# Four pairs instead of three in two w_down passes, a pair's sums over raw blocks, and the first loads of x

## The chip, the cores and the metric

The kernel runs on one core of one Trainium2 chip. Its metric is device time in microseconds, the median of several executions. Beside that there is one execution taken by the hardware profiler, from which all rows of the profile come.

## The reference

One layer of a streaming encoder, float32, 256 tokens of 2048 channels:

```python
xn = rms_norm(h, norm1_g)
proj = xn @ w_in                       # 2048 x 5120: q, k, v, two conv halves
att = diff_attention(q, k, v, lam)     # 4 heads, block-causal, then rms_norm
u = silu(layer_norm(conv31(ga * sigmoid(gg))))
h = h + concat(att, u) @ w_out         # 2048 x 2048
hn = rms_norm(h, norm2_g)
h = h + (silu(hn @ w_gate) * (hn @ w_up)) @ w_down     # hidden width 5632
```

The five weight matrices hold 49 million numbers, some 200 MB. Each is read from HBM while it is used.

## The kernel before

**Products in three terms.** Every float32 operand is split into a high part (rounded to fp32r by ScalarE) and a low part (what is left, by VectorE). A product takes three matmuls: high by high, low by high, high by low. One matmul is 128x128 by 128x512.

**Two kinds of unit in the feed-forward half.** The gate and up products run in blocks j = 0 to 10 of 512 hidden columns, and w_down runs in three passes, behind j=3, j=7 and j=10, since the hidden activations are multiplied as they come. A pass has two w_down blocks, each over two groups of 512 output columns. From j=1 on, all these blocks are made of units, which an order string such as `sgGsgGsUUsUu` lists:

- A plain unit (g or u) takes two 128-row slices of one weight matrix for both halves of the tokens: 12 matmuls. In a lower-case unit VectorE makes the low part of the weights (L351). In an upper-case unit ScalarE writes the negated weights (L345), and a DMA of GpSimd adds the raw weights on top (L346).
- A pair unit (s) takes the 2x2 blocks of two slices by two column groups and multiplies them with seven products instead of eight, in the way of Strassen and Winograd: 7 x 3 = 21 matmuls, where a g and a u unit would need 24. For it the four weight blocks b are loaded in one DMA of 1 MB (`load_pair`, L1051), VectorE forms four sums t (`pair_sums`, L1057 to L1059), ScalarE rounds three raw blocks (`round_raw`, L1064) and the four sums (`round_pair`, L1068), and VectorE makes the low parts of both (`split_pair`, L1072 and L1073). The matmuls are lines 1090 to 1092, those of plain units 1112 and 1117. The activation side has its own seven forms; for w_down they are made by `pair_forms` (L965 to L980), while a plain unit of w_down only needs a high and a low part (L953, L955).

**Banks.** A block sums into eight PSUM banks. Seven products go into seven of them. When a block's last pair is done, a generator is started that forms the results from them (`bank_sums`, L1194 to L1199, on VectorE). It enters the instruction streams at the next `resume()`, of which there are two in a plain unit and four in a pair unit. The next block's first pair writes the same banks, in the order Q6, Q7, Q5, Q1, Q2, Q4, Q3, and must wait until they have been read. The last two banks are read by L1213 (gate and up) or L1247 (w_down).

**Order of issue.** `run_chunks` writes the instruction streams by hand. Ahead of unit t it issues, in this sequence: the low parts up to unit t+3; the raw rounding of pairs up to t+5, if the pair two before lies ahead of t; the pairs' sums up to t+5; the units with a DMA low part up to t+5; the rounding up to t+4; and the loads up to t+9. Then come the unit's matmuls. Each engine and each queue works its stream off in order. A pair's blocks b have two buffers (and so have its high and its low parts), its sums t have one, plain raw weights have four.

**Orders.** Block j=1 has `gugusGsUsGsU`, since its activation forms are made at the last moment, blocks j=2 to 10 have `sgGsgGsUUsUu`, and the w_down blocks of the first two passes `sgGsgGgsuUuUu`. In a pass of w_down the pairs of the list in `DOWN` are pairs of slices (j, half); the other slices are plain.

**The start.** SP's queue loads the weights chunk by chunk, and ahead of chunk c the c-th part of x. Only the head (gains and part 0) and part 1 come through ScalarE's queue. Chunks 0 to 3 are half as wide as the others. Chunks up to 9 share the four raw buffers.

Of the kernel before, what the change touches and what calls it, by code (L numbers as in the profile page):

```python
# [13 lines left out]
F32 = mybir.dt.float32  # L14
F32R = mybir.dt.float32r
# [4 lines left out]
P = 128  # L20
# [65 lines left out]

Q1, Q6, Q7, Q5, Q2, Q4, Q3, QX = range(8)

PRODUCTS = ((Q6, 5, 1), (Q7, 6, 2), (Q5, 4, 3), (Q1, 0, 5), (Q2, 1, 6), (Q4, 2, 0), (Q3, 3, 4))

DOWN = (dict(pairs=((1, 0), (1, 1), (2, 0)), order=("sgGsgGgsuUuUu",) * 2),
        dict(pairs=((4, 0), (4, 1), (5, 0)), order=("sgGsgGgsuUuUu",) * 2),
        dict(pairs=((8, 0), (8, 1), (9, 0)), order=("sGsGgsUUu", "sGsGGsUUu")))

RAW_AHEAD = 5
LOAD_AHEAD, DMA_AHEAD, SUMS_AHEAD, HI_AHEAD, LO_AHEAD = 9, 5, 5, 4, 3


BLOCKS = 2 * KD + 1

TO_TRANSPOSE = 5

# [12 lines left out]
def tile_block(  # L115
# [46 lines left out]
    head = pre.tile([P, NK * N], F32, tag="lod", name="head", bufs=1)[:, : NR + S]  # L162
    act.dma_start(out=head, in_=xt[:, : NR + S])
    x_load(XPARTS[1], act)
    pool.tensor_scalar(cols, head[:, :NR], 1.0, 0.0, ALU.mult, ALU.add)

    act.copy(small.tile([P, 8], F32, tag="rsq", name="first"), neghalf)
# [156 lines left out]
    def load_chunk(c):  # L324
        view = lambda t: t.rearrange("p (k n) -> p k n", n=c["width"])[:, : c["nk"]]
        c["view"] = view
        if c.get("spare_raw"):
            c["raw"] = view(early.tile([P, 4 * N], F32, tag="wb", name="raw")[:, : NK * N])
        else:
            c["raw"] = view(wp.tile([P, NK * N], F32, tag="raw", name="raw", bufs=RAW_BUFS))  # L330
        ks = c["ks"] if "ks" in c else range(c["k0"], c["k0"] + c["nk"])
        c["src"] = src = weights([(c["w"], k, col, n) for k in ks for col, n in c["cols"]])
        sp.dma_start(out=c["raw"].rearrange("p k n -> p (k n)"), in_=src)
# [73 lines left out]
            start(c["done"](ps))  # L407

    loaded, rounded, parted = [0], set(), set()
    pair_at, two_at = [], []  # L410

    def earlier(at, i, n):
# [61 lines left out]
    def run_chunks():  # L474
        n = len(chunks)
        pair_at.extend(i for i, c in enumerate(chunks) if "sides" in c)
        two_at.extend(i for i, c in enumerate(chunks) if "kind" in c and "sides" not in c)
        at = dict(part=0, dma=0, sums=0, round=0, minus=0, raw=0)
        first = next(i for i, c in enumerate(chunks) if "kind" in c)

        def until(what, do, stop, only=lambda c: True, may=lambda i: True):
            while at[what] < min(n, stop) and may(at[what]):
                if only(chunks[at[what]]):
                    do(at[what])
                at[what] += 1

        for t in range(n):
            if t >= first - AHEAD:
                until("part", part_of, t + 1 + LO_AHEAD)
                until("raw", lambda i: round_raw(chunks[i]), t + 1 + RAW_AHEAD, lambda c: "sides" in c,  # L490
                      lambda i: i <= t or may_round_raw(t, i))
                until("sums", sums_of, t + 1 + (SUMS_AHEAD if t >= first else 0), may=may_sum)
                until("dma", round_of, t + 1 + DMA_AHEAD, lambda c: c["by_dma"])
                until("round", round_of, t + 1 + (HI_AHEAD if t >= first else LO_AHEAD))
                load_until(t + 1 + LOAD_AHEAD)
            else:
                if t < len(XPARTS):
                    until("part", part_of, t + 2)
                else:
                    until("part", part_of, t + 1 + AHEAD)  # L500
                    until("minus", minus_of, min(t + 1 + MINUS_AHEAD, first), lambda c: c.get("minus"))
                    until("round", round_of, min(t + 1 + ROUND_AHEAD, first))
            part_of(t)
            chunks[t]["multiply"](chunks[t])
            if chunks[t].get("prompt") and chunks[t]["done"]:
                resume()
        while running:
            resume()
# [331 lines left out]
    def out_done(n, ps):  # L840
        cs = slice(n * N, (n + 1) * N)
        for m in range(NM):
            dve.tensor_tensor(h[m][:, cs], h[m][:, cs], ps[m], ALU.add)
        for m in range(NM):
            pool.dma_start(out=out[m * P : (m + 1) * P, cs], in_=h[m][:, cs])
        if n == 2:
            held[0] -= NM
        yield
        for t in range(0, N // P, 2):
            k = n * (N // P) + t  # L850
            yield from room(1)
            pt = aux_ps.tile([P, 2, S], F32, tag="aux", name="ps_h")
            for i in range(2):
                for m in range(NM):
                    pe.transpose(pt[:, i, m * P : (m + 1) * P], h[m][:, (k + i) * P : (k + i + 1) * P], ident)
            if k % HK == 0:
                hn.append(early.tile([P, HK, S], F32, tag="wb", name="hn"))
            rows = hn[k // HK][:, k % HK : k % HK + 2, :]
            for i in range(2):
                act.activation(rows[:, i, :], pt[:, i, :], AF.Copy, scale=col("g2", k + i))  # L860
            hi, lo = lhs_two("h", k)
            act.copy(hi, rows)
            dve.tensor_tensor(lo, rows, hi.bitcast(F32), ALU.subtract)
            for i in range(2):
                hT[k + i] = (hi[:, i, :], lo[:, i, :])
            yield
        for m in range(NM):
            square_sum(h[m][:, cs], ss2[m][:, n : n + 1])
        if n == D // N - 1:
            yield  # L870
            for m in range(NM):
                ss = small.tile([P, 1], F32, tag="ssh", name="ssh")
                dve.tensor_reduce(ss, ss2[m], AX.X, ALU.add)
                rsqrt_mean(rstd2[m], ss, D, EPS)
            yield
            yield
            prestack.close()
            ffn["pool"] = fp = ctx.enter_context(tc.tile_pool(name="ffn", bufs=1))
            spare_lhs.extend(fp.tile([P, 2, 2, S], F32R, tag=f"a{x}", name=f"a{x}") for x in ("hi", "lo"))
            start(make_forms())  # L880


# [40 lines left out]
    def place(g):  # L923
# [3 lines left out]
        fhi, flo = (a[:, :at].rearrange("p (f q) c -> p f q c", f=7) for a in arena)  # L927
        twos = [(j, t) for j in range(sum(FGROUPS[:g]), sum(FGROUPS[: g + 1])) for t in range(2) if (j, t) not in pairs]
        free = [arena_two(i) for i in range(at, BLOCKS - 3, 4)]
        free += [tuple(a[:, i] for a in spare_lhs) for i in range(2)]  # L930
        assert len(free) >= len(twos)
        down[g] = dict(forms=(fhi, flo), pairs=pairs, twos=twos, at=dict(zip(twos, free)), ready=set())

# [107 lines left out]
    def load_pair(c):  # L1041
        if "b" in c:
            return
        queue = sp
        if c is chunks[pair_at[0]]:
            c["b"] = ffn["pool"].tile([P, 7, N], F32, tag="wl", name="wb0", bufs=2)[:, :4]
            queue = pool
        else:
            c["b"] = early.tile([P, 4, N], F32, tag="wb", name="wb")
        src = weights([(w, k, col, N) for w, col in c["sides"] for k in c["ks"]])  # L1050
        queue.dma_start(out=c["b"].rearrange("p k n -> p (k n)"), in_=src)  # L1051

    def pair_sums(c):

        b = c["b"]
        c["t"] = t = ffn["pool"].tile([P, 4, N], F32, tag="wt", name="wt")
        dve.tensor_tensor(t[:, 2:4], b[:, 1:3], b[:, 0:1].to_broadcast([P, 2, N]), ALU.subtract)  # L1057
        dve.tensor_tensor(t[:, 1], b[:, 1], t[:, 3], ALU.add)
        dve.tensor_tensor(t[:, 0], t[:, 1], b[:, 3], ALU.subtract)  # L1059

    def round_raw(c):
        if "hi" not in c:
            c["hi"] = ffn["pool"].tile([P, 7, N], F32R, tag="wh", name="wh", bufs=2)
            act.copy(c["hi"][:, 4:], c["b"][:, 1:])  # L1064

    def round_pair(c):
        round_raw(c)
        act.copy(c["hi"][:, :4], c["t"])  # L1068

    def split_pair(c):  # L1070
        c["lo"] = ffn["pool"].tile([P, 7, N], F32R, tag="wl", name="wl", bufs=2)
        dve.tensor_tensor(c["lo"][:, 4:], c["b"][:, 1:], c["hi"][:, 4:].bitcast(F32), ALU.subtract)  # L1072
        dve.tensor_tensor(c["lo"][:, :4], c["t"], c["hi"][:, :4].bitcast(F32), ALU.subtract)  # L1073

    def sum_bank(c, i):
        sums = c["sums"]
# [145 lines left out]
    def down_products(n, q, last):  # L1222
        so_far = None
        if last:
            so_far = ffn["pool"].tile([P, 4, N], F32, tag="wt", name="so_far")[:, :NM]
            pool.dma_start(out=so_far, in_=out[:, n * N : (n + 1) * N].rearrange("(m p) n -> p m n", p=P))
        bank_sums(q)
        for m in range(NM):
# [42 lines left out]
    for ks, first, last in ((range(0, 4), True, False), (range(4, 6), False, False), (range(6, 8), False, False),  # L1271
                            (range(8, 16), False, True)):
        for n in range(3):
            block("w_out", n * N, ks, fm, (lambda ps, n=n: out_done(n, ps)) if last else None,
                  bkey=("o", n), first=first, last=last, spare=n == 2)
    block("w_out", 3 * N, range(16), fm, lambda ps: out_done(3, ps))
    for i, c in enumerate(chunks[len(XPARTS) : -12]):
        c["spare_raw"] = i % 3 == 2
        c["minus"] = i >= MINUS_FROM and i % 6 == 4
# [12 lines left out]
        j0 += nb  # L1292

    for c, part in enumerate(XPARTS):
        before[c] = lambda c=c, part=part: (x_load(part, sp) if c > 1 else None, x_part(part))
    before[H_FROM + NM - 1] = lambda part=XPARTS[H_FROM + NM - 1]: (x_load(part, sp), x_part(part), start(x_rest()))
    for i in range(2 * NM):
        x_first = before.get(H_FROM + i, lambda: None)
# [40 lines left out]
```

## Time and profile before

| | us |
|---|---|
| median of 3 executions (lowest, highest) | 1037.16 (1037.03, 1037.67) |
| the profiled execution's own time | 1037.66 |
| its span in the profile | 1035.9 |
| granted TensorE clock over the span | 1.00 |
| busy: TensorE, its weight loads, VectorE, ScalarE, GpSimd | 1028.0, 849.0, 862.7, 685.8, 155.1 |

In rows of the profile PE is TensorE, PEld its weight loads, DVE VectorE, ACT ScalarE, POOL GpSimd, and SPq the DMA queue of SyncE. `L1072` is line 1072 of the kernel. A row of the timeline gives start and duration in us, engine, line, operation, output and inputs, shapes, count, and in brackets the idle time of the engine ahead of it with what ended it. Stretches (windows) are in us from the start of the span.

### The profile page before, as it was taken

What the parts mean: (1) busy time and instruction counts of PE and PEld (TensorE: products, weight loads), DVE (VectorE), ACT (ScalarE), POOL (GpSimd) and SP (SyncE); (2) the same over time, 40 slices, a digit from 0 to 9 for tenths busy, and PEclk for the clock granted to TensorE, in tenths of its full rate; (3) what the DMA queues carried; (4) which work ended last, traced back from release to release, by engine and by line L of the source; (5) the groups of instructions that cost most, each with busy time, mean ns of one, the idle gap of its engine ahead of it and who ended that gap; (6) DMA issues with size and microseconds to landing.
All of it is one profiled execution on the core that took longest, in us unless ns stands there. A gap on an engine that the chain in (4) does not pass through costs nothing.

```text
span 1035.9 us, 13050 instructions
## 1 busy us (share of the span) xinstructions
PE 1028.0 (99%) x4641; PEld 849.0 (82%) x4641; DVE 862.7 (83%) x1087; ACT 685.8 (66%) x865; POOL 155.1 (15%) x198
## 2 busy tenths in 40 slices
PE   9999999999999999999999999999999999999998
PEld 7888888888888888788888888888888888888886
DVE  6699889897646699999978779999896697998983
ACT  6855567767756577777566667776765666767761
POOL 0040232411100101011011111110101121111121
PEclk9999999999999999999999999999999999999999
DMA  9967775676566669798889998987969999889896
GB/s 341 326 201 239 236 208 187 189 218 183 154 211 224 229 238 262 247 319 240 254 255 292 260 308 263 307 237 241 309 186 286 290 283 327 234 250 299 238 263 130
DMA packets 66065, 258.05 MB, mean 249 GB/s; under 512 B 7376, under 2 KB 8912, under 8 KB 58576
## 3 DMA queue, kind: packets, MB, share of 16 engines
q1 hardware_dynamic: 48944, 201.34, 53.7%
q0 software_dynamic: 16768, 55.58, 28.2%
q8 instruction: 36, 0.59, 0.2%
q10 hardware_dynamic: 288, 0.29, 0.1%
q14 instruction: 29, 0.24, 0.1%
HBM read 248.80 MB, written 8.39 MB: 248 GB/s over the span
## 4 chain that ended last, share of the span: by engine, by line
PE 83%; DVE 9%; DMA 3%; POOL 2%; ACT 1%; issue 1%; DVEq 0%; ACTq 0%
PE q L1112 23%; PE q L1117 12%; PE q L1090 9%; PE q L1091 9%; PE q L1092 9%; PE acc L387 6%; PE acc L381 6%; PE acc L382 6%; DVE y L592 5%; DVE wlo L351 3%; DMA raw<-in_wts_dram 3%; PE ps_a L918 1%; POOL rsq L220 1%; PE ps_s L727 1%; PE ps_o L805 1%
## 5 line engine op out<-in xcount | busy, mean ns | idle before, releaser
L342 ACT CAST whi<-raw 128x1024 fp32r<-128x1024 f32 (+1 forms) x262 | 270.5, 1042 | 102.8 <-PE acc L382 44.4
L351 DVE TENSOR_TENSOR wlo<-raw,whi 128x1024 fp32r<-128x1024 f32 (+1 forms) x174 | 209.1, 1210 | 71.4 <-ACT whi L342 68.4
L381 PE MATMUL acc<-whi,lhi 128*128 128x512 f32 x416 | 164.2, 395 | 1.2 <-ACT whi L342 1.2
L382 PE MATMUL acc<-whi,llo 128*128 128x512 f32 x416 | 162.2, 390 | 0.0
L1073 DVE TENSOR_TENSOR wl<-wt,wh 128x2048 fp32r<-128x2048 f32 x58 | 132.7, 2287 | 20.2 <-ACT wh L1068 20.1
L1064 ACT CAST wh<-wb 128x1536 fp32r<-128x1536 f32 x58 | 86.0, 1484 | 86.9 <-PE q L1091 54.0
L346 POOL DMA_DIRECT2D wlo<-in_wts_dram x74 | 65.1, 891 | 509.7 <-ACT wlo L345 486.0
L1068 ACT CAST wh<-wt 128x2048 fp32r<-128x2048 f32 x58 | 110.5, 1904 | 18.5 <-DVE wt L1059 18.4
L1090 PE MATMUL q<-wh,fhi 128*128 128x512 f32 x280 | 109.1, 390 | 0.4 <-DVE sum L1197 0.4
L1092 PE MATMUL q<-wl,fhi 128*128 128x512 f32 x280 | 109.0, 389 | 0.0
L1091 PE MATMUL q<-wh,flo 128*128 128x512 f32 x280 | 108.9, 389 | 0.0
L1072 DVE TENSOR_TENSOR wl<-wb,wh 128x1536 fp32r<-128x1536 f32 x58 | 101.6, 1751 | 2.1 <-ACT wh L1064 2.1
L592 DVE SCALAR_TENSOR_TENSOR y<-upad,cw,y 128x256 f32<-128x256 f32 x240 | 100.5, 481 | 3.2 <-ACT y L585 3.2
L387 PE MATMUL acc<-wlo,lhi 128*128 128x512 f32 x368 | 100.7, 395 | 0.5 <-DVE wlo L351 0.5
L381 PEld LDWEIGHTS acc<-whi,lhi 128*128 128x128 f32 x416 | 78.1, 188 | 18.4 <-ACT whi L342 2.3
L382 PEld LDWEIGHTS acc<-whi,llo 128*128 128x128 f32 x416 | 78.2, 188 | 16.0
L1117 PE MATMUL q<-wlo,chi 128*128 128x512 f32 x320 | 86.9, 393 | 0.0
L1112 PE MATMUL q<-whi,chi 128*128 128x512 f32 x320 | 85.8, 390 | 0.0
L1112 PE MATMUL q<-whi,clo 128*128 128x512 f32 x320 | 85.6, 389 | 0.0
L387 PEld LDWEIGHTS acc<-wlo,lhi 128*128 128x128 f32 x368 | 68.4, 188 | 14.6 <-DVE wlo L351 0.9
L345 ACT ACTIVATE wlo<-raw 128x1024 fp32r<-128x1024 f32 x74 | 78.2, 1056 | 0.0
L1057 DVE TENSOR_TENSOR wt<-wb 128x1024 f32<-128x1024 f32 x58 | 70.8, 1220 | 2.0 <-DMA wb<-in_wts_dram 1.6
(224 smaller groups left out, 1682.0 us busy)
## 6 DMA issues: line engine op xcount, KB each, us to landing
raw<-in_wts_dram SPq DMA_DIRECT2D x258, 512.0 KB, 5.6
wb<-in_wts_dram SPq DMA_DIRECT2D x57, 1024.0 KB, 7.9
wlo<-in_wts_dram POOLq DMA_DIRECT2D x74, 512.0 KB, 9.3
lod<-in_wts_dram POOLq DMA_DIRECT2D x14, 512.0 KB, 6.4
out_dram<-sum POOLq DMA_DIRECT2D x22, 256.0 KB, 7.2
h<-in_x_dram SPq DMA_DIRECT2D x4, 512.0 KB, 9.1
out_dram<-h POOLq DMA_DIRECT2D x8, 256.0 KB, 3.7
xt<-in_xt_dram SPq DMA_DIRECT2D x6, 256.0 KB, 6.8
```

The lines of the kernel that those rows point to most:

```text
L342: act.copy(c["hi"], c["raw"])
L351: dve.tensor_tensor(c["lo"], c["raw"], c["hi"].bitcast(F32), ALU.subtract)
L381: pe.matmul(ps[m], xhi[:, ms], hi[:, j, :], start=c["first"] and j == 0, stop=False)
L382: pe.matmul(ps[m], xlo[:, ms], hi[:, j, :], start=False, stop=False)
L387: pe.matmul(ps[m], xhi[:, ms], lo[:, j, :], start=False, stop=c["last"] and j == nk - 1)
L592: dve.scalar_tensor_tensor(y[:, ct, :], src, wk, y[:, ct, :], ALU.mult, ALU.add)
L1073: dve.tensor_tensor(c["lo"][:, :4], c["t"], c["hi"][:, :4].bitcast(F32), ALU.subtract)
L1090: pe.matmul(ps, fhi[:, f, p, :], c["hi"][:, w], start=bool(first), stop=False)
L1091: pe.matmul(ps, flo[:, f, p, :], c["hi"][:, w], start=False, stop=False)
L1092: pe.matmul(ps, fhi[:, f, p, :], c["lo"][:, w], start=False, stop=bool(last))
L1112: pe.matmul(ps, plain[i][e][:, ms], hi[:, i, :], stop=False, start=i == e == 0 and bool(c["first"].get(qs[m])))
L1117: pe.matmul(sum_bank(c, qs[m]), plain[i][0][:, ms], lo[:, i, :], start=False, stop=i == 1 and bool(c["last"].get(qs[m])))
```

## The change

- `DOWN`: the first two passes of w_down have four pairs each, the slices of j=1 and j=2 (and of j=4 and j=5) in both halves, where the second half of j=2 (and of j=5) was plain. The order becomes `sgGsgGsuUsUu`: 4 pair units and 8 plain units, for 3 and 10. Each column group keeps two lower-case and two upper-case plain units, where it had three and two.
- A pair's sums: only two of the four go into t (which is half as big). The third is written over the raw block b[0], and the fourth over b[1], after that block has been rounded and split. For it the blocks are loaded in another order, and the seven forms of the weights stand at other places (`PRODUCTS`). The split of the three raw blocks with the fourth sum is a function of its own, `split_raw`. It is issued with the rounding, if the pair two before stands ahead of the current unit, and with the rest of the split otherwise. The rounding of the four sums becomes two casts, one of t and one of b[0] and b[1], and their split becomes two operations.
- Memory: the space that t gives up goes to a third spare buffer for plain activations (`SPARE`), and the arena of activation parts is one block shorter.
- The start: parts 2 and 3 of x are loaded in one DMA on ScalarE's queue, and the raw weights of chunks 4 and 5 go to the space of v, which is not yet in use then.

```diff
-PRODUCTS = ((Q6, 5, 1), (Q7, 6, 2), (Q5, 4, 3), (Q1, 0, 5), (Q2, 1, 6), (Q4, 2, 0), (Q3, 3, 4))
-
-DOWN = (dict(pairs=((1, 0), (1, 1), (2, 0)), order=("sgGsgGgsuUuUu",) * 2),
-        dict(pairs=((4, 0), (4, 1), (5, 0)), order=("sgGsgGgsuUuUu",) * 2),
+PRODUCTS = ((Q6, 5, 2), (Q7, 6, 0), (Q5, 4, 1), (Q1, 0, 6), (Q2, 1, 4), (Q4, 2, 3), (Q3, 3, 5))
+
+DOWN = (dict(pairs=((1, 0), (1, 1), (2, 0), (2, 1)), order=("sgGsgGsuUsUu",) * 2),
+        dict(pairs=((4, 0), (4, 1), (5, 0), (5, 1)), order=("sgGsgGsuUsUu",) * 2),
         dict(pairs=((8, 0), (8, 1), (9, 0)), order=("sGsGgsUUu", "sGsGGsUUu")))
...
-BLOCKS = 2 * KD + 1
+BLOCKS = 2 * KD
+
+SPARE = 3
...
     x_load(XPARTS[1], act)
+    x_load(range(2, 4), act)
...
+        elif "raw_tag" in c:
+            c["raw"] = view(pre.tile([P, NK * N], F32, tag=c["raw_tag"], name="raw", bufs=1))
...
-        src = weights([(w, k, col, N) for w, col in c["sides"] for k in c["ks"]])
+        blocks = [(w, k, col, N) for w, col in c["sides"] for k in c["ks"]]
+        src = weights([blocks[i] for i in (0, 3, 1, 2)])
...
     def pair_sums(c):
         b = c["b"]
-        c["t"] = t = ffn["pool"].tile([P, 4, N], F32, tag="wt", name="wt")
-        dve.tensor_tensor(t[:, 2:4], b[:, 1:3], b[:, 0:1].to_broadcast([P, 2, N]), ALU.subtract)
-        dve.tensor_tensor(t[:, 1], b[:, 1], t[:, 3], ALU.add)
-        dve.tensor_tensor(t[:, 0], t[:, 1], b[:, 3], ALU.subtract)
+        c["t"] = t = ffn["pool"].tile([P, 2, N], F32, tag="wt", name="wt")
+        dve.tensor_tensor(t, b[:, 2:], b[:, 0:1].to_broadcast([P, 2, N]), ALU.subtract)
+        dve.tensor_tensor(b[:, 0], b[:, 2], t[:, 1], ALU.add)
...
+    def split_raw(c):
+        if "lo" not in c:
+            b = c["b"]
+            c["lo"] = ffn["pool"].tile([P, 7, N], F32R, tag="wl", name="wl", bufs=2)
+            dve.tensor_tensor(c["lo"][:, 4:], b[:, 1:], c["hi"][:, 4:].bitcast(F32), ALU.subtract)
+            dve.tensor_tensor(b[:, 1], b[:, 0], b[:, 1], ALU.subtract)
+
     def round_pair(c):
         round_raw(c)
-        act.copy(c["hi"][:, :4], c["t"])
+        act.copy(c["hi"][:, :2], c["t"])
+        o = earlier(pair_at, c["at"], 2)
+        if o is None or o < now[0]:
+            split_raw(c)

     def split_pair(c):
-        c["lo"] = ffn["pool"].tile([P, 7, N], F32R, tag="wl", name="wl", bufs=2)
-        dve.tensor_tensor(c["lo"][:, 4:], c["b"][:, 1:], c["hi"][:, 4:].bitcast(F32), ALU.subtract)
-        dve.tensor_tensor(c["lo"][:, :4], c["t"], c["hi"][:, :4].bitcast(F32), ALU.subtract)
+        split_raw(c)
+        act.copy(c["hi"][:, 2:4], c["b"][:, :2])
+        dve.tensor_tensor(c["lo"][:, :2], c["t"], c["hi"][:, :2].bitcast(F32), ALU.subtract)
+        dve.tensor_tensor(c["lo"][:, 2:4], c["b"][:, :2], c["hi"][:, 2:4].bitcast(F32), ALU.subtract)
...
+    for m in range(NM):
+        chunks[RAW_BUFS + m]["raw_tag"] = f"v{m}"
...
-        before[c] = lambda c=c, part=part: (x_load(part, sp) if c > 1 else None, x_part(part))
+        before[c] = lambda c=c, part=part: (x_load(part, sp) if c > 3 else None, x_part(part))
```

More of the change, by code (lines that the diff above doesn't have):

```diff
@@ L409, in tile_block @@
     loaded, rounded, parted = [0], set(), set()
+    now = [0]
     pair_at, two_at = [], []
@@ L485, in until @@
                 at[what] += 1
+        for i in pair_at:
+            chunks[i]["at"] = i
         for t in range(n):
+            now[0] = t
             if t >= first - AHEAD:
@@ L878, in out_done @@
             ffn["pool"] = fp = ctx.enter_context(tc.tile_pool(name="ffn", bufs=1))
-            spare_lhs.extend(fp.tile([P, 2, 2, S], F32R, tag=f"a{x}", name=f"a{x}") for x in ("hi", "lo"))
+            spare_lhs.extend(fp.tile([P, SPARE, 2, S], F32R, tag=f"a{x}", name=f"a{x}") for x in ("hi", "lo"))
             start(make_forms())
@@ L929, in place @@
         free = [arena_two(i) for i in range(at, BLOCKS - 3, 4)]
-        free += [tuple(a[:, i] for a in spare_lhs) for i in range(2)]
+        free += [tuple(a[:, i] for a in spare_lhs) for i in range(SPARE)]
         assert len(free) >= len(twos)
@@ L1224, in down_products @@
         if last:
-            so_far = ffn["pool"].tile([P, 4, N], F32, tag="wt", name="so_far")[:, :NM]
+            so_far = ffn["pool"].tile([P, NM, N], F32, tag="wt", name="so_far")
             pool.dma_start(out=so_far, in_=out[:, n * N : (n + 1) * N].rearrange("(m p) n -> p m n", p=P))
```

## The prediction

> **What bounds the kernel now.** I read the waits of TensorE first, because the page has it busy nearly throughout. The columns are total us, times, longest.
>
> ```profile
> PE acc L381 <- ACT whi L342: 1.2, 2, 0.8
> PE acc L387 <- DVE wlo L351: 0.5, 1, 0.5
> PE q L1090 <- DVE sum L1197: 0.4, 1, 0.4
> PE q L1112 <- DVE llo L955: 0.2, 1, 0.2
> ```
>
> Once the first matmul has started, the profile shows 2.3 us of waiting in the whole span. The rest is matmuls handed over without a break, and their pitch has to be read from starts, since the ends are modelled. TensorE's timeline in block j=1, one pair unit and the unit of one product group behind it:
>
> ```profile
> 396.22 0.39 PE L1090 MATMUL q<-wh,fhi 128*128 128x512 f32 x1
> ...
> 400.98 1.07 PE L1112 MATMUL q<-whi,chi 128*128 128x512 f32 x4
> ...
> 403.70 0.39 PE L1090 MATMUL q<-wh,fhi 128*128 128x512 f32 x1
> ```
>
> The pair: 4.76 us for 21 matmuls. The plain unit: 2.72 us for 12. Both give 0.2267 us a matmul. So fewer matmuls save their pitch, and any stall that VectorE or ScalarE puts in front of TensorE is added whole. For the question who can do that, the load of VectorE by stage (columns: us, then busy us and count of PE, PEld, DVE, ACT, POOL, granted clock, DMA share, GB/s); the rows are blocks j=2, the first w_down block, and j=5:
>
> ```profile
> 426.14:468.67 42.53, 42.11 (x189) 34.42 (x188) 41.77 (x52) 30.37 (x32) 4.31 (x5) 1.00 0.90 270
> 510.44:552.88 42.44, 42.44 (x192) 35.13 (x191) 33.71 (x34) 26.64 (x25) 5.28 (x6) 1.00 0.80 227
> 635.16:676.93 41.77, 41.77 (x189) 34.58 (x188) 39.60 (x48) 30.52 (x33) 4.33 (x5) 1.00 0.87 265
> ```
>
> In j=2 VectorE is busy 41.77 of 42.53 us, and it is the block at whose start TensorE waits for the bank sums (L1197). There is no reserve there.
>
> **Part 1, the fourth pair.** Each of the four changed w_down blocks has 3 pairs and 10 plain units now (63 + 120 matmuls), then 4 and 8 (84 + 96): 3 matmuls fewer, 12 in all, 12 x 0.2267 = **-2.7 us**. All lie on the path. The Trainium skill (Perfetto Trace Analysis, Identifying the Most-Contended Engine) holds matmul occupancy for a poor measure and judges TensorE by its weight-load time; by the 34.58 us of weight loads for 188 matmuls in the j=5 row, 12 of them would be worth 2.2 us. The starts decide here, so I stay with 2.7.
>
> **Part 2, the pair's preparation.** VectorE's timeline at the end of block j=1 has every operation of a pair once:
>
> ```profile
> 414.40 1.22 DVE L1057 TENSOR_TENSOR wt<-wb 128x1024 f32<-128x1024 f32 x1
> 415.66 0.69 DVE L1058 TENSOR_TENSOR wt<-wb,wt 128x512 f32<-128x512 f32 x1
> 416.38 0.69 DVE L1059 TENSOR_TENSOR wt<-wt,wb 128x512 f32<-128x512 f32 x1
> 417.48 1.76 DVE L1072 TENSOR_TENSOR wl<-wb,wh 128x1536 fp32r<-128x1536 f32 x1 [0.40 <-ACT wh L1064]
> 419.29 2.29 DVE L1073 TENSOR_TENSOR wl<-wt,wh 128x2048 fp32r<-128x2048 f32 x1
> 422.13 1.23 DVE L351 TENSOR_TENSOR wlo<-raw,whi 128x1024 fp32r<-128x1024 f32 x1 [0.55 <-ACT whi L342]
> 423.27 1.22 DVE L1057 TENSOR_TENSOR wt<-wb 128x1024 f32<-128x1024 f32 x1
> ...
> 425.86 0.68 DVE L1194 TENSOR_TENSOR sum<-q,sum 128x512 f32<-128x512 f32 x1
> ...
> 428.05 0.68 DVE L1197 TENSOR_TENSOR sum<-q,sum 128x512 f32<-128x512 f32 x1
> ```
>
> Now a pair costs 1.22 + 0.69 + 0.69 + 1.76 + 2.29 = 6.65 us of VectorE. After, the sum L1059 moves behind the raw split and L1073 becomes two 128x1024 splits, priced by L351 (1.23): 1.22 + 0.69, then 1.76 + 0.69, then 2 x 1.23, together 6.82. For 58 pairs that is +10 us of VectorE, four more pairs +27, eight plain splits fewer -10. A changed w_down block goes from 33.7 to about 38 us in some 41; a gate-and-up block gains about 0.7. Most of it is covered by VectorE's idle time (2.2 us in j=5). The extra pair's forms for j=2 and j=5 add about 2 us to VectorE in j=3 and j=6, where j=5, which already makes two pairs' forms, shows the room.
>
> What matters is not the sum but the place. The raw split and the moved sum (1.76 + 0.69 = 2.45 us) are now put in VectorE's queue with the rounding, four units ahead, if the pair two before has had its matmuls issued; the sums of the seven banks are put there only at a resume inside the unit behind the last pair. In the order with four pairs that unit is the 11th and the early split that could stand in front belongs to unit 15, rounded at 11: behind the bank sums. In block j=1 (order gugusGsUsGsU) the last pair is unit 10, so its bank sums enter inside unit 11, and the early split of unit 15 (the second pair of j=2) enters **before** them. The row 428.05 is what TensorE waits for:
>
> ```profile
> 428.79 0.51 PE L1090 MATMUL q<-wh,fhi 128*128 128x512 f32 x1 [0.42 <-DVE sum L1197]
> ```
>
> Second, the pairs of units 8, 10 and 12 stand only two units apart, so their split isn't early: raw split, moved sum, and only then ScalarE's cast of b's two blocks, which now waits for VectorE with ScalarE's later casts behind it. ScalarE's timeline there:
>
> ```profile
> 415.96 1.49 ACT L1064 CAST wh<-wb 128x1536 fp32r<-128x1536 f32 x1 [3.92 <-PE q L1091]
> 417.35 1.91 ACT L1068 CAST wh<-wt 128x2048 fp32r<-128x2048 f32 x1
> 419.16 1.04 ACT L342 CAST whi<-raw 128x1024 fp32r<-128x1024 f32 x1
> 420.11 1.06 ACT L345 ACTIVATE wlo<-raw 128x1024 fp32r<-128x1024 f32 x1
> 421.07 1.03 ACT L342 CAST whi<-raw 128x1024 fp32r<-128x1024 f32 x1
> ```
>
> L1064 at 415.96 is held by TensorE and doesn't move. L1072 starts at 417.48 as now, the moved sum ends at 417.48 + 1.76 + 0.69 = 419.9, the cast of the two blocks lasts to 421.0 (1.05, as L342), and the three casts behind it begin 1.8 us later than now (421.0 for 419.16). So L351 starts 1.8 later; the sums behind it are shorter by 0.69; the early split adds 2.45. The bank sums move by 1.8 - 0.69 + 2.45 = 3.6 us, and so does TensorE: **+3.6 us** at 428.79. The low end is 1.8 (2.45 - 0.69, if ScalarE keeps its times), the high end 4.4: a pair's blocks are now read until its last split, so the next load into them, and the loads behind it in SP's queue, go out later by up to 0.69 + 2.29 us, and one cast in this block already waits for its load. Of the 3.0 us, 1.22 us of ScalarE's idle time and the 0.40 and 0.55 us of VectorE's above take up the most, and 0.8 is left:
>
> ```profile
> 405.25 1.06 ACT L342 CAST whi<-raw 128x1024 fp32r<-128x1024 f32 x1 [0.20 <-DMA raw<-in_wts_dram]
> ...
> 408.48 1.49 ACT L1064 CAST wh<-wb 128x1536 fp32r<-128x1536 f32 x1 [1.22 <-issue]
> ```
>
> **Part 3, forms that are needed sooner.** With (2,1) a pair, the w_down block after j=3 needs the forms of (3,0) and (3,1) as units 4 and 5, for 5 and 6 now: 2.7 us sooner. VectorE writes the last of them here,
>
> ```profile
> 525.79 0.68 DVE L955 TENSOR_TENSOR alo<-ps_a,ahi 128x512 fp32r<-128x512 f32 x1
> ```
>
> and TensorE begins unit 5 and comes to its low part, in an order whose first five units stay as they are:
>
> ```profile
> 529.08 1.07 PE L1112 MATMUL q<-whi,ahi 128*128 128x512 f32 x4
> 529.99 1.07 PE L1112 MATMUL q<-whi,alo 128*128 128x512 f32 x4
> ```
>
> These are the places where (3,1) will be read. VectorE ends the bank sums at about the block's start, 510.1 (window row 510.44). Behind them it will have an early split (2.45), four bank operations of the old block (2.4), two late splits (2.5), a plain split (1.2), the sums of the pair in unit 6 (1.9), its early split (2.45), a form (0.7), its late splits (2.5), a plain split (1.2), and the sums of the pair in unit 9 (1.9), 19.2 us to 529.3; the form itself takes 0.7, to 530.0. Nothing is left over. I take 0.3 us for each of the first and second pass and 0.2 for the third pass's start, where the row L955 of the waits already stands and an early split comes ahead of the bank sums: **+0.8 us**, from 0 to 4.
>
> **Part 4, the start.** SP's queue, ScalarE and TensorE around the first wait, and the DMA share (the number before the last) in two stretches:
>
> ```profile
> 4.38 0.33 SPq L159 DMA_DIRECT2D xt<-in_xt_dram  x1
> 4.38 0.51 ACT L243 ACTIVATE lhi<-head 128x256 fp32r<-128x256 f32 x1 [1.25 <-DMA head<-in_xt_dram]
> ...
> 6.15 0.33 SPq L333 DMA_DIRECT2D raw<-in_wts_dram  x1
> ...
> 10.93 1.05 ACT L342 CAST whi<-raw 128x1024 fp32r<-128x1024 f32 x1 [1.93 <-DMA raw<-in_wts_dram]
> ...
> 12.03 0.50 PE L381 MATMUL acc<-whi,lhi 128*128 128x512 f32 x1 [0.84 <-ACT whi L342]
> ```
> ```profile
> 7.00:8.00 1.00, 1.00 (x6) 0.84 (x5) 1.00 (x3) 1.00 (x3) 0.00 (x0) 1.00 0.75 172
> ...
> 16.00:18.00 2.00, 2.00 (x10) 1.65 (x10) 1.58 (x4) 1.90 (x4) 0.00 (x0) 1.00 1.03 413
> ```
>
> The load issued at 6.15 is chunk 4's; it stood waiting for a raw buffer, while the DMA engines ran out of work (0.75). With v's space it need not wait. Of x's parts 2 and 3, two issues leave SP's queue, past the loads of chunks 2 to 4, and one is added to ScalarE's, some 0.4 us; ScalarE's 1.25 us wait for the head of x covers it, and without that wait it would move the first cast by that 0.4. So chunk 4 lands over 1 us sooner and the 0.84 us wait of TensorE goes. But the loads behind it keep the DMA engines full (1.03 in the second stretch), so only the idle share up to there is really won, some 0.6 us. The Trainium skill (DMA: Bandwidth & Descriptors, Issuing engines are not separate DMA queues) says that issuing from another engine saves its issue time alone; by that the x part is worth nothing here and the gain is the buffer's. I take **-0.6 us**, from -1.3 to 0: in the chain that ended last VectorE stands between these rows,
>
> ```profile
> 46.93 0.95 DVE y L592 x3
> ...
> 163.40 1.21 PE acc L387 x4
> ```
>
> and if it came no sooner there, the one wait of L387 for VectorE (0.5) would grow by what the start gives.
>
> **The sum.** -2.7 + 3.6 + 0.8 - 0.6 = +1.1 us. The profiled execution took 1037.66 us for its span of 1035.9, 0.5 above the median; with the median, 1037.16 + 1.1 = 1038.2 us.
>
> **The rivals.** *Faster: the bank sums keep their place.* If VectorE reaches L1194 behind j=1 no later than now, the sum is -2.7 - 0.6 + 0.8 = -2.5, or -3.3 with no stall in part 3: 1033.9 to 1034.7 us. For it: VectorE's 0.40 and 0.55 us waits in the rows above show some give. Against it: the order of issue, which no duration changes.
>
> *Slower: the blocks are held longer.* From the DMA page:
>
> ```profile
> wb<-in_wts_dram SPq DMA_DIRECT2D x57, 1024.0 KB, 7.9
> ```
>
> The load of a pair's blocks takes 7.9 us and starts when the pair two before is split. Moved by up to 3 us, it makes VectorE wait wherever its blocks now land less than that ahead of the sums. It decides once these waits outrun the time by which the low parts are ready ahead of TensorE; in the two blocks with nothing to spare (j=2, and a w_down block with 38 us of work) it would cost a late load's 2.5 us once: +3.6, 1040.8 us. Against it: in the j=5 row the DMA engines have room (0.87).
>
> *Slower: part 3 at its upper end*, 2 us in each of two passes: 1.1 - 0.6 + 4 = +4.5, 1041.7 us.
>
> **Chances.** The forecast 0.46 (own range 1035.2 to 1039.3, from the low ends of parts 2 and 4 with 0.2 for part 3 to the high end of part 2 with 0.3 won at the start), the kept place 0.25, the held blocks 0.17, part 3 0.12. Faster or slower means by more than 0.2% (2.1 us), about what a measurement of this kernel can tell from no change: 0.25 faster, 0.46 the same, 0.29 slower. The range, 1033.8 to 1041.2 us, takes in the faster case and the first slower one.
>
> **What would show it.** The page should count 12 matmuls fewer. There should be a wait of L1090 for the bank sums' L1197 near 428 us of about 4 us in place of 0.4 (0.82 between starts), with the raw split of a pair just ahead of L1194; no wait of 0.8 us near 12 us; small waits for L955 in the w_down blocks. If L1194 follows directly on the pair sums as now, part 2 is wrong and the time falls below 1035. If VectorE waits for the pairs' loads in many places, the held blocks decide.

## The result

| | before | after |
|---|---|---|
| median of 5 executions (lowest, highest), us | 1037.16 (1036.94, 1037.67) | 1060.57 (1058.46, 1061.97) |
| span of the profiled execution, us | 1035.9 | 1058.3 |
| matmuls in the trace | 4641 | 4629 |
| busy: VectorE, ScalarE, us | 862.7, 685.8 | 886.9, 696.8 |

The changed kernel is slower: 1.0216 times the time before, with a 95% interval of 1.0205 to 1.0227. That is 23.4 us, far above the forecast of 1038.2 and outside the range, which ended at 1041.2.

### The profile page after: what moved, and what is told of

It is laid out like the page before. It is cut to its first block, busy times and chain, and to the rows that moved or that the text cites. A ratio compares the mean times of both kernels' runs of the same rounds, so it can differ in the third digit from the quotient of the medians.

```text
span 1058.3 us, 13183 instructions
## 1 busy us (share of the span) xinstructions
PE 1033.6 (98%) x4629; PEld 847.0 (80%) x4629; DVE 886.9 (84%) x1173; ACT 696.8 (66%) x933; POOL 154.0 (15%) x198
## 5 line engine op out<-in xcount | busy, mean ns | idle before, releaser
L347 ACT CAST whi<-raw 128x1024 fp32r<-128x1024 f32 (+1 forms) x254 | 262.0, 1040 | 64.7 <-PE acc L387 44.6
L356 DVE TENSOR_TENSOR wlo<-raw,whi 128x1024 fp32r<-128x1024 f32 (+1 forms) x166 | 199.6, 1211 | 75.7 <-ACT whi L347 74.8
L1091 ACT CAST wh<-wb 128x1024 fp32r<-128x1024 f32 x62 | 65.1, 1050 | 97.4 <-DVE wb L1080 97.4
L1073 ACT CAST wh<-wb 128x1536 fp32r<-128x1536 f32 x62 | 91.8, 1480 | 49.0 <-PE q L1111 23.6
L1110 PE MATMUL q<-wh,fhi 128*128 128x512 f32 x280 | 111.3, 397 | 11.8 <-DVE sum L1233 5.7
L1079 DVE TENSOR_TENSOR wl<-wb,wh 128x1536 fp32r<-128x1536 f32 x62 | 108.6, 1751 | 4.4 <-ACT wh L1073 4.3
L1132 PE MATMUL q<-whi,chi 128*128 128x512 f32 x320 | 86.7, 393 | 0.0
L1132 PE MATMUL q<-whi,clo 128*128 128x512 f32 x320 | 86.3, 392 | 0.0
L1067 DVE TENSOR_TENSOR wt<-wb 128x1024 f32<-128x1024 f32 x62 | 75.6, 1219 | 10.5 <-DMA wb<-in_wts_dram 10.5
L1092 DVE TENSOR_TENSOR wl<-wt,wh 128x1024 fp32r<-128x1024 f32 x62 | 75.6, 1219 | 5.8 <-ACT wh L1084 5.8
```

The costliest lines, as they stand in the source:

```text
L347: act.copy(c["hi"], c["raw"])
L356: dve.tensor_tensor(c["lo"], c["raw"], c["hi"].bitcast(F32), ALU.subtract)
L1079: dve.tensor_tensor(c["lo"][:, 4:], b[:, 1:], c["hi"][:, 4:].bitcast(F32), ALU.subtract)
L1110: pe.matmul(ps, fhi[:, f, p, :], c["hi"][:, w], start=bool(first), stop=False)
L1132: pe.matmul(ps, plain[i][e][:, ms], hi[:, i, :], stop=False, start=i == e == 0 and bool(c["first"].get(qs[m])))
```

## The profile after

The waits of TensorE in the changed kernel (total us, times, longest). In it `bank_sums` is L1214 to L1219, and the last two banks are read by L1233 (gate and up) or L1267 (w_down).

```profile
PE q L1110 <- DVE sum L1233: 8.9, 9, 1.9
PE q L1110 <- DVE sum L1214: 4.8, 2, 4.5
PE q L1132 <- DVE alo L964: 1.4, 2, 0.7
...
PE q L1110 <- DVE sum L1267: 1.2, 4, 0.3
PE ps_a L927 <- DVE alo L964: 0.9, 2, 0.5
PE acc L386 <- ACT whi L347: 0.9, 2, 0.7
PE q L1110 <- DVE sum L1217: 0.7, 2, 0.4
PE ps_a L927 <- DVE llo L964: 0.4, 1, 0.4
PE acc L392 <- DVE wlo L356: 0.2, 1, 0.2
```

They come to 19.4 us, where the waits of before came to 2.3 (the first matmul's own start is left out in both). The wait for L1214 was forecast. The largest row, L1233, was not: nine times a pair waits until VectorE has read the last two banks of the block before. Four waits for L1267 are the same thing in w_down.

The time closes. For every 512-column matmul the trace has a start. What each start lies beyond 0.227 us behind the one before it adds up to 10.2 us before and to 34.9 us after: 24.7 more. Twelve matmuls fewer give 2.7 back, which leaves 22.0 of the 22.4 us by which the span of the profiled execution grew (the medians differ by 23.4). Of the 24.7 us, 19.9 lie at waits and 4.8 in matmuls that follow each other at a longer pitch (the last section says where most of those are).

Why is VectorE late? The waits of ScalarE and VectorE of the changed kernel. L1080 is the fourth sum, written over b[1], L1091 the cast of b[0] and b[1], L347 the cast of a plain unit's weights and L356 their split:

```profile
ACT wh L1091 <- DVE wb L1080: 97.4, 48, 6.1
DVE wlo L356 <- ACT whi L347: 74.8, 55, 3.9
...
ACT wh L1073 <- DMA wb<-in_wts_dram: 20.4, 5, 5.9
...
DVE wt L1067 <- DMA wb<-in_wts_dram: 10.5, 5, 4.5
```

ScalarE waits for the fourth sum at 48 of the 62 pairs, 97.4 us in all. That row doesn't exist before. VectorE's wait for a plain unit's cast does, with 68.4 us, so its total has hardly grown; what matters is where it falls. Over the whole of block j=2 the profile before shows no wait of VectorE, and the changed kernel shows 4.8 us of this one, in three waits. The place where one block ends and the next begins shows what it does. VectorE, ScalarE and TensorE in turn at the end of j=5 of the changed kernel, from the timeline:

```profile
678.40 1.06 ACT L1091 CAST wh<-wb 128x1024 fp32r<-128x1024 f32 x1 [2.73 <-DVE wb L1080]
679.36 1.04 ACT L347 CAST whi<-raw 128x1024 fp32r<-128x1024 f32 x1
680.30 1.05 ACT L350 ACTIVATE wlo<-raw 128x1024 fp32r<-128x1024 f32 x1
681.26 1.03 ACT L347 CAST whi<-raw 128x1024 fp32r<-128x1024 f32 x1
...
682.32 1.23 DVE L356 TENSOR_TENSOR wlo<-raw,whi 128x1024 fp32r<-128x1024 f32 x1 [1.61 <-ACT whi L347]
...
689.07 0.68 DVE L1219 TENSOR_TENSOR sum<-q,sum 128x512 f32<-128x512 f32 x1
689.67 1.75 DVE L1079 TENSOR_TENSOR wl<-wb,wh 128x1536 fp32r<-128x1536 f32 x1
691.45 0.69 DVE L1080 TENSOR_TENSOR wb<-wb 128x512 f32<-128x512 f32 x1
692.06 1.28 DVE L1233 TENSOR_TENSOR sum<-q,sum 128x512 f32<-128x512 f32 x2
...
692.80 0.50 PE L1110 MATMUL q<-wh,fhi 128*128 128x512 f32 x1 [0.61 <-DVE sum L1233]
```

Two things meet. First, ScalarE's 2.73 us of waiting push three casts, the split L356 then waits 1.61 us for the last of them, and everything VectorE does behind it is that much later. Second, between the bank sums (L1219) and the reading of the last two banks (L1233) there now stands the early split of a pair that is needed four units later, 2.45 us. Before, at the same place, L1233's counterpart followed the bank sums at once:

```profile
675.86 0.68 DVE L1199 TENSOR_TENSOR sum<-q,sum 128x512 f32<-128x512 f32 x1
676.68 1.29 DVE L1213 TENSOR_TENSOR sum<-q,sum 128x512 f32<-128x512 f32 x2
...
676.93 0.39 PE L1090 MATMUL q<-wh,fhi 128*128 128x512 f32 x1
```

There the pair began at 676.93 and came to bank Q3, behind 18 matmuls, at 681.01. The bank was free near 677.3, half way through the two operations of L1213: 3.7 us to spare. After, the same pair comes to it 4.08 us behind its start at 687.95, at 692.03, while L1233 only starts at 692.06.

In w_down the two things feed each other. The start of a w_down block near 560 us in the changed kernel, VectorE and then ScalarE:

```profile
561.21 1.75 DVE L1079 TENSOR_TENSOR wl<-wb,wh 128x1536 fp32r<-128x1536 f32 x1
563.00 0.69 DVE L1080 TENSOR_TENSOR wb<-wb 128x512 f32<-128x512 f32 x1
563.61 1.28 DVE L1267 TENSOR_TENSOR sum<-q,sum 128x512 f32<-128x512 f32 x2
...
563.72 1.05 ACT L1091 CAST wh<-wb 128x1024 fp32r<-128x1024 f32 x1 [6.06 <-DVE wb L1080]
```

The early split stands behind the six bank sums, as the prediction said, but ScalarE's cast waits for it there, and so waits for the bank sums too, 6.06 us.

## The experiments

Two theories for the 22 us of the span. **Cast:** ScalarE's cast of b[0] and b[1] must wait for the raw split and the sum that VectorE writes over b[1]; the casts behind it come late, and so do VectorE's splits and bank operations. **Place:** the early split is simply put ahead of bank operations that TensorE waits for, and its 2.45 us are paid at each block's start. The rival of the held blocks (late loads) was still open too. The kernel before ran beside each group, with medians of 1037.79, 1037.69 and 1037.68 us.

**The start alone.** The kernel before with part 4 of the change (`x_load(range(2, 4), act)` and `raw_tag`), nothing else.

> The kernel before with the change of the start alone (x's parts 2 and 3 on ScalarE's queue, chunks 4 and 5 in v's space). The profile of the changed kernel has block j=1 begin 1.3 us sooner (first plain matmul at 386.6 for 388.0). If that gain lasts to the end: 1037.2 - 1.3 = 1035.9 us. By the prediction's term: 1036.6. If VectorE's chain swallows it: 1037.2.

1036.88 us, 0.9992 of before (0.9983 to 1.0001). TensorE's waits:

```profile
PE acc L390 <- DVE wlo L354: 0.9, 1, 0.9
PE acc L384 <- ACT whi L345: 0.6, 1, 0.6
PE q L1093 <- DVE sum L1200: 0.4, 1, 0.4
```

The 0.84 us wait at 12.03 is gone, and the wait of the low part's matmul for VectorE (near 162 us) has grown from 0.5 to 0.9, as the prediction feared for the end of its range at nothing. About 0.9 us is left, and the interval just includes nothing.

**The preparation without the fourth pair.** The changed kernel with the passes of before.

```diff
-DOWN = (dict(pairs=((1, 0), (1, 1), (2, 0), (2, 1)), order=("sgGsgGsuUsUu",) * 2),
-        dict(pairs=((4, 0), (4, 1), (5, 0), (5, 1)), order=("sgGsgGsuUsUu",) * 2),
+DOWN = (dict(pairs=((1, 0), (1, 1), (2, 0)), order=("sgGsgGgsuUuUu",) * 2),
+        dict(pairs=((4, 0), (4, 1), (5, 0)), order=("sgGsgGgsuUuUu",) * 2),
```

> The changed kernel with the first two w_down passes as before (three pairs, old orders), so with the new preparation of the pairs and the new start alone. Theory 'preparation': the waits at the ends of blocks stay (in the changed kernel's trace about 20 us stand at the gate-and-up blocks, 4 to 6 in the w_down blocks); about 1037.2 - 1.3 + 20 = 1056 us. Rival 'fourth pair': the denser passes are to blame, and the time falls back to 1036 to 1038 us.

1058.75 us, 1.0202 (1.0181 to 1.0223). The loss is in the preparation, not in the fourth pair, whose 12 matmuls fewer don't show either (1060.57 with it). The waits are the same ones:

```profile
PE q L1110 <- DVE sum L1233: 7.4, 9, 1.7
PE q L1110 <- DVE sum L1214: 4.7, 1, 4.7
```

**No early split.** The changed kernel with the split of the raw blocks always at the pair's other splits.

```diff
         act.copy(c["hi"][:, :2], c["t"])
-        o = earlier(pair_at, c["at"], 2)
-        if o is None or o < now[0]:
-            split_raw(c)
```

> The changed kernel without the early raw split: split_raw is issued with the rest of the split for every pair. Theory 'place' (2.45 us of VectorE stand ahead of the bank operations): these waits go, about 1060.6 - 13 = 1047 us or less, and L1233 no longer holds TensorE. Theory 'cast' (ScalarE's cast of the blocks waits for the moved sum, 97 us in all, and its later casts and so VectorE come late): every pair now meets this wait in full, and the time stays at 1058 us or above.

1074.89 us, 1.0357 (1.0339 to 1.0376): worse by another 14 us. With the split out of the way of the bank operations, TensorE's waits for L1233 nearly go (its line is L1230 here, 0.9 us), and those for the first bank sum fall from 4.8 to 1.2 us, as "place" said. But ScalarE waits half as much again, and TensorE for what ScalarE delivers late, the low parts that GpSimd's DMA completes. TensorE's waits and ScalarE's:

```profile
PE q L1134 <- DMA wlo<-in_wts_dram: 11.7, 8, 2.2
PE q L1129 <- DVE alo L964: 4.1, 2, 2.0
PE q L1129 <- ACT ahi L962: 2.7, 2, 1.4
...
PE q L1107 <- DVE sum L1230: 0.9, 1, 0.9
```
```profile
ACT wh L1088 <- DVE wb L1080: 144.2, 55, 7.2
```

So the early issue is what kept ScalarE's wait short, and L1233's waits need both: a late VectorE and the early split ahead of the reading. "Place" alone falls.

**The early split behind the unit's matmuls.** As in the last experiment, but `split_raw` is issued after the unit's resumes, so that the bank operations go first.

```diff
             if chunks[t].get("prompt") and chunks[t]["done"]:
                 resume()
+            for i in pair_at:
+                o = earlier(pair_at, i, 2)
+                if i in rounded and i not in parted and (o is None or o <= t):
+                    split_raw(chunks[i])
```

> The changed kernel with the early raw split issued behind the unit's matmuls and resumes instead of ahead of them: the bank operations stand ahead of it in VectorE's queue, and it still precedes the cast by an order of issue. Theory 'place': most of the waits at block ends go, 1043 us or less. Theory 'cast': ScalarE waits still longer for the moved sum, and the time stays at 1056 us or above.

1076.08 us, 1.0369 (1.0354 to 1.0385), with the same picture: ScalarE's cast waits 145.4 us for the fourth sum, 56 times. But this edit changes nothing. Ahead of unit t pairs up to t+4 are rounded, and ahead of unit t+1 the low parts up to t+4 come first of all, so a split issued at the end of unit t stands where it stood. In the traces of this and of the last experiment VectorE's 1173 operations come in the same order, and so do ScalarE's 933 and TensorE's 4629 matmuls. The two times are two measurements of one program, 1.2 us apart. What a place behind the bank operations but well ahead of the cast would give stays untested.

**The cast at another place on ScalarE's queue.** The changed kernel, early split kept, but a pair's late cast and late splits are issued behind the unit's other casts.

```diff
-                until("part", part_of, t + 1 + LO_AHEAD)
+                until("part", part_of, t + 1 + LO_AHEAD, lambda c: "sides" not in c)
...
                 until("round", round_of, t + 1 + (HI_AHEAD if t >= first else LO_AHEAD))
+                for i in pair_at:
+                    if i <= t + LO_AHEAD:
+                        part_of(i)
```

> After, with one move on ScalarE's queue: a pair's cast of b's first two blocks (which waits for VectorE's moved sum) and its late splits are issued behind the unit's other casts, not ahead of them. Theory 'cast' (ScalarE waits about 1.2 to 2.7 us for the moved sum at nearly every pair, and the casts behind it, the plain units' low parts and so VectorE's bank operations come later by that): most of the +22 us goes, 1040 to 1050. Theory 'place' (VectorE's queue alone is too long ahead of the bank operations): it stays at 1056 or more, as the early split keeps its place.

1050.4 us, 1.012 (1.0105 to 1.0135). Some 10 of the 22 us are back: less than the "most" that "cast" forecast, just above its range, and well below the 1056 of "place". ScalarE's wait for the sum falls from 97.4 to 15.3 us (12 times), and TensorE keeps these:

```profile
PE q L1113 <- DVE sum L1236: 5.3, 4, 1.7
PE q L1113 <- DVE sum L1217: 3.1, 1, 3.1
PE q L1113 <- DVE sum L1270: 2.5, 1, 2.5
```

They are the bank operations again (L1236 and L1270 read the last two banks, L1217 begins the bank sums), so the place may still have a share, or a pair's late casts and splits are now late themselves; this run can't tell the two apart.

**The dependency removed.** Passes of three pairs; the fourth sum is formed at once into a third block of t, so that no cast waits for the raw split. Only the third sum stays in b[0]. The early split (now 1.75 us) keeps its place.

```diff
-        c["t"] = t = ffn["pool"].tile([P, 2, N], F32, tag="wt", name="wt")
-        dve.tensor_tensor(t, b[:, 2:], b[:, 0:1].to_broadcast([P, 2, N]), ALU.subtract)
+        c["t"] = t = ffn["pool"].tile([P, 3, N], F32, tag="wt", name="wt")
+        dve.tensor_tensor(t[:, :2], b[:, 2:], b[:, 0:1].to_broadcast([P, 2, N]), ALU.subtract)
         dve.tensor_tensor(b[:, 0], b[:, 2], t[:, 1], ALU.add)
+        dve.tensor_tensor(t[:, 2], b[:, 0], b[:, 1], ALU.subtract)
...
-            dve.tensor_tensor(b[:, 1], b[:, 0], b[:, 1], ALU.subtract)
...
-        act.copy(c["hi"][:, 2:4], c["b"][:, :2])
+        act.copy(c["hi"][:, 3], c["b"][:, 0])
```

> After with the passes of three pairs and with the fourth sum formed at once in pair_sums, in a third block of t, so that b[1] is not written over: no cast waits for the raw split any more, only the third sum stays in b[0]. The early raw split (1.76 us) keeps its place. Theory 'cast': back to before or nearly, 1036 to 1040. Theory 'place' (the early split ahead of the bank operations costs by itself): 1.75 of the 2.45 us are still there, 1046 or more.

1040.57 us, 1.0028 (1.0017 to 1.0038). Against the kernel with the preparation of the change and the same three pairs (1.0202), one block more in t takes back nearly all: 0.6 us above the range of "cast", far below the 1046 of "place". The edit also gives back the third spare buffer for activations and puts two of the seven forms at other places; the kernel with four pairs below keeps that buffer, and there the same step takes the changed kernel from 1060.57 to 1037.89. ScalarE's wait for the moved sum is gone from its rows; for the sums in t it waits 13.1 us, where it waited 18.4 before. What is left of TensorE's waits:

```profile
PE q L1110 <- DVE sum L1214: 2.2, 1, 2.2
...
PE acc L386 <- ACT whi L347: 0.5, 1, 0.5
PE acc L392 <- DVE wlo L356: 0.5, 1, 0.5
PE q L1110 <- DVE sum L1233: 0.4, 1, 0.4
```

**The same without the early split.** The three lines that call `split_raw` early are left out as above.

> The kernel with the fourth sum in t, without the early raw split: the raw split stands at the pair's other splits as in the kernel before. The difference to the kernel with the early split is the price of its place alone. Theory 'cast': 1036 to 1040, within 2 us of the one with the early split. Theory 'place': 1036 to 1040 here too, but 8 us or more below the one with the early split. If a pair's blocks, which are still read by its last split, decide: 1045 or more in both.

1037.55 us, 1.0000 (0.9990 to 1.0010): 3.0 us below, more than the 2 that "cast" allowed and far less than the 8 of "place". The wait for the bank sums behind j=1 falls back from 2.2 to 0.5:

```profile
PE acc L392 <- DVE wlo L356: 0.7, 1, 0.7
PE q L1107 <- DVE sum L1211: 0.5, 1, 0.5
PE q L1107 <- DVE sum L1214: 0.4, 1, 0.4
```

With ScalarE's wait gone, the place costs 3.0 us, by the rows at one spot: the bank sums behind j=1, where the wait is 1.7 us longer and a slower clock follows it (last section). The kernel has the start of the change, worth 0.9, so the preparation may still cost about that much. The held blocks are out as the cause as well. In this kernel b[0] is read until the pair's last split, as in the changed one. And the waits of VectorE and ScalarE for the loads of pairs don't go with the time: 30.9 us together in the changed kernel, 16.9 in the slower one without the early split, 30.5 in the one with the cast moved, 21.2 and 19.3 in the two fast ones with four pairs that follow.

**The fourth pair on top.** The kernel with the dependency removed and the early split, with the passes of the change.

> The kernel with the fourth sum in t and the early split, with the passes of four pairs of the change (the DMA scratch is cut by half to make room). 12 matmuls fewer are worth 2.7 us; the forms that are needed sooner cost about 3 by the waits of the trace after (0.8 by the prediction). So 0 to 2 us below the kernel with three pairs by the prediction's terms, 0 to 1 above it by the trace's. With theory 'cast' 1034 to 1041, with 'place' 1044 or more.

1037.89 us, 1.0004 (0.9995 to 1.0014), 2.7 us below the kernel with three pairs (1.0028), as much as 12 matmuls. The wait of L1132 for the forms that are needed sooner, 1.4 us in the changed kernel, is 0.2 here.

**What is worth having.** The dependency removed, no early split, four pairs, and the start.

> The fourth sum in t, no early raw split, the passes of four pairs, the start of the change: what the runs leave as worth having. If the terms add (2.7 for the fourth pair as between the two kernels with the early split, 3.0 for the split's place as between the two with three pairs): 1034.9, ratio 0.997. If the forms that are needed sooner only find VectorE too late in the four-pair passes: 1036 to 1037.5, no gain over the kernel with three pairs.

1035.37 us, 0.9978 (0.9969 to 0.9987): faster than the kernel before by 0.2%, and near the 1034.9 at which the terms add up. It is 2.2 us below the kernel with three pairs and no early split.

## Why the prediction was wrong

**Part 1 (12 matmuls, -2.7 us) was right.** The page counts 12 fewer, and the pair of runs with and without the fourth pair differs by 1040.57 - 1037.89 = 2.7 us, the other such pair, without the early split, by 1037.55 - 1035.37 = 2.2. By the weight loads, as the page of the Trainium skill weighs it, it would have been 2.2; the intervals, some 1 us to each side, don't tell the two apart. In the changed kernel itself the gain is lost among the waits.

**Part 2 is the step that failed,** in the sentence "Most of it is covered by VectorE's idle time" and in costing the place at one boundary only. Its +3.6 us measured 21.9: 1058.75 with the preparation and the start of the change, 1036.88 with the start alone. What it said of that boundary held nearly to the digit:

```profile
423.98 1.22 DVE L356 TENSOR_TENSOR wlo<-raw,whi 128x1024 fp32r<-128x1024 f32 x1 [1.62 <-ACT whi L347]
...
426.98 1.75 DVE L1079 TENSOR_TENSOR wl<-wb,wh 128x1536 fp32r<-128x1536 f32 x1
428.77 0.69 DVE L1080 TENSOR_TENSOR wb<-wb 128x512 f32<-128x512 f32 x1
429.38 0.68 DVE L1214 TENSOR_TENSOR sum<-q,sum 128x512 f32<-128x512 f32 x1
...
430.12 0.50 PE L1110 MATMUL q<-wh,fhi 128*128 128x512 f32 x1 [4.47 <-DVE sum L1214]
```

The raw split and the moved sum stand just ahead of L1214, ScalarE's casts make L356 late, L1214 starts 3.5 us later than L1194 did for the 3.6 forecast, and the wait is 4.47 us for "about 4". What the prediction left out there is the clock: from the start of the pair to the next unit TensorE takes 11.18 us (424.80 to 435.98) for 5.52 before. Of these 5.7 us, 4.0 lie at the wait, and most of the rest behind it, where the clock is halved (last section). But the greater part lies elsewhere: the same two mechanisms work at the ends of the later blocks too, and there the prediction had no price for them. It made two errors. It looked for the early split ahead of the bank *sums* only, found it behind them in the other orders, and stopped; the two operations behind the sums, on which the next pair's last product waits, were not followed, though before they had only 3.7 us to spare. And it priced ScalarE's wait for the moved sum only for pairs two units apart in j=1, while the row of 97.4 us shows it at 48 of 62 pairs.

The amount of VectorE's work was right: +27 us forecast, 886.9 - 862.7 = +24.2 measured. The cover was not. In block j=2 of the changed kernel (us, then busy us and count of PE, PEld, DVE, ACT, POOL, granted clock, DMA share, GB/s)

```profile
424.80:473.00 48.20, 43.73 (x190) 35.44 (x188) 44.32 (x58) 31.89 (x37) 4.30 (x5) 0.96 0.85 260
```

VectorE has more idle time than before in that block (44.32 of 48.20 us busy, for 41.77 of 42.53), and is later. Its idle time is spent waiting for ScalarE's casts, which come late because ScalarE waits for VectorE. Such idle time covers nothing.

**Part 3 (+0.8 us)** was too small, within its range of 0 to 4. The rows of waits for the forms (L964) come to 2.7 us in the changed kernel: two of 0.7 us where L1132 reads them, for the 0.3 taken, and 1.3 at L927. With three pairs they are 0.5. The last form starts at 529.67 where the prediction's count came to 529.3. With four pairs and the dependency gone only 0.2 us is left, so they were mostly the same lateness.

**Part 4 (-0.6 us)** came to about -0.9, within its range. How much of it is the raw buffers and how much the queue of x's parts was not tried, so the rule on issuing engines that the prediction cites stays untested.

**The rivals.** "The bank sums keep their place" fell with the 4.47 us. "The blocks are held longer" has its sign in the profile (loads make VectorE wait 10.5 us and ScalarE 20.4), but kernels that read them until the last split too, with 11.4 to 21.2 us of such waits, are as fast as before. The end that came, a wait in a ring of two engines at 48 of 62 pairs, was not among the rivals, though the prediction named the wait itself.

## What to carry to other kernels

When an edit makes engine A wait for engine B, and B's later work waits for A, price it at every place where it occurs, and don't set the idle time of either engine against it. Follow each operation that is put ahead in a queue to the last consumer behind it, not only to the first one that comes to mind: here the bank sums were looked at and the two bank readings behind them were not. And a buffer saved by writing over an input can cost far more than the work it moves: one block of 512 columns more in t was worth some 18 us with three pairs and 22.7 with four.

## What the runs showed of the hardware

The wait of 4.47 us cost more than itself. TensorE's granted clock (the number behind the five engines) ahead of it and behind it, in the changed kernel:

```profile
421.20:425.20 4.00, 4.00 (x19) 3.34 (x18) 2.38 (x3) 4.00 (x5) 0.87 (x1) 1.00 0.78 269
430.90:434.30 3.40, 3.40 (x9) 2.52 (x9) 3.40 (x6) 1.55 (x3) 0.00 (x0) 0.50 0.43 139
434.40:436.40 2.00, 2.00 (x10) 1.68 (x9) 2.00 (x4) 2.00 (x3) 0.00 (x0) 1.00 0.00 0
```

For 3.4 us the clock is half, and matmuls start 0.43 us apart in place of 0.227, which adds 1.8 us to the wait. A wait of 2.16 us at the same place in the kernel with the dependency removed did the same (1.7 us more), and so did one of 1.86 us at 908.15 in the changed kernel. The two stretches in the changed kernel make some 3.6 of the 4.8 us that it loses to longer pitches. The kernel without the early split has five stretches of 3.4 us at 0.50 or 0.51, behind waits of 1.84 to 2.21 us, so that some 5 of the 14 us by which it is slower are the clock. Length alone doesn't decide: another wait of 1.86 us, at 650.1, and one of 3.07 us in the kernel with the cast moved, cost only 0.2 to 0.3 us behind them, and no wait of up to 1.7 us cost more than 0.3. The Trainium skill (TensorE: Matmul & The Clock Gate, Part 1 on the clock gate) gives 426.7 ns for such a matmul at half the clock, which agrees, and a free-running window of about 3.4 us of idleness ahead of it. That the outcome varies for equal waits fits a free-running window; that 1.86 us of waiting were enough is shorter than the page says.
